# Depthwise convolution taps split into ScalarE products and 1024-column VectorE additions in a two-layer hybrid decoder trunk

## The chip, the cores and the metric

One core of a Trainium2 chip runs the whole program. The metric is the device time of one execution in microseconds (us). Engines are written as in the profile: PE is TensorE (PEld its weight loads), DVE is VectorE, ACT is ScalarE, POOL is GpSimd and SP is SyncE, which issues most loads.

## What is computed

Two layers, each a pre-normalised mixer with three branches that read the same input, then one output projection into the residual; at the end a last RMS norm. Sequence 256, width 2048, everything float32.

```python
h = rms_norm(x, norm_w)
proj = h @ w_in
(qa, ka, va, za, qi, ki, wi, ub, zb, qc, kc, vc, zc, gates) = jnp.split(proj, split_points(), axis=-1)
...
y_a = (dsa_attention(qa, ka, va, qi, ki, wi, top_k) * jax.nn.silu(za)) @ w_a_out
y_b = (conformer_conv(ub, conv_w, conv_b, cln_w, cln_b) * jax.nn.silu(zb)) @ w_b_out
...
y_c = (stick_breaking_attention(qc, kc, vc) * jax.nn.silu(zc)) @ w_c_out
merged = g[:, :, 0] * y_a + g[:, :, 1] * y_b + g[:, :, 2] * y_c
return x + merged @ w_out
```

Branch B is the one that the change touches:

```python
def conformer_conv(u, conv_w, conv_b, ln_w, ln_b):
    a, gt = jnp.split(u, 2, axis=-1)
    y = a * jax.nn.sigmoid(gt)
    y = lax.conv_general_dilated(y, conv_w.astype(y.dtype), window_strides=(1,),
                                 padding=[(CONV_WIDTH - 1, 0)],
                                 dimension_numbers=('NWC', 'WIO', 'NWC'),
                                 feature_group_count=CONV_CH) + conv_b
    y = layer_norm(y, ln_w, ln_b)
    return jax.nn.silu(y)
```

The convolution is depthwise and causal, 31 taps wide, over 1024 channels: for each channel, 31 shifted copies of a row of 256 time steps, each times one weight, are added up, and a bias with them.

## The kernel before

**Weight units.** All projections stream their weights through SBUF in units of 128 partitions x 1024 columns. `load_unit` issues the load on SP into one of five `raw` buffers. `high` (L251, ACT) casts the unit to the matmul's rounded type: `wh`. `low` (L255, DVE) subtracts that from `raw` and so gets the remainder `wl`; `split` uses the same two lines on activations (names `ph`, `pl`, `s`), and L584 and L585 are the two lines for narrower tiles. Three buffers of `wh` and three of `wl` exist. For each unit PE runs 8 matmuls with `wh` and 4 with `wl`, of 512 columns, mostly into `acc` (L265).

**Order of the work.** The program is written out in the order of the units; each counts up `count[0]`. The tile framework orders each engine's instructions from it, and sets the waits between engines. Work that is not projections (norms, rotary embedding, index scores, top-k, softmax, gates) is put between the units: `background` calls generators at a count that each of them names, `tails` and `pending` do the same for work that is due by a certain unit, and `issue_after` ties an instruction behind the newest cast, subtraction or matmul. An engine runs its own instructions in order: whatever stands ahead of a cast or of a subtraction holds it.

**The taps.** The gated input of the convolution lies in `yT` with channels on partitions: 8 channel tiles of 128 channels x (30 zeros + 256 steps). `cv` holds the result, 128 x 8 x 256. `tap` (L645, L647) is one DVE instruction for one channel tile and one tap: it multiplies the shifted row by the weight's column and adds the result in place. `use_u(0)` and `use_u(1)`, one for each half of the channels, put 124 taps each on the list `waiting` in groups of one or two; `drain`, called by `low` after each subtraction, issues one group behind that subtraction. While the index queries are projected (from the line `hold[0] = True` until the projection of the attention queries has been written) `drain` gives out nothing. `flush` empties the list ahead of the layer norm, `conv_norm`.

**The norm of the convolution.** `conv_norm` sums `cv` over its 8 channel tiles with two reductions (L1305) and an addition, lets PE sum over partitions, subtracts the mean, squares on ACT, sums again in two reductions (L1316), and then scales, adds a bias and gates: `AF.Sigmoid` on ACT (L1330), scale and bias on DVE (L1331).

**Later uses named below.** L1034 and L1035 find the largest index scores of each query. L1078 holds the index score matmuls that read the split index query. L1256 is an exponential of the stick-breaking branch, L1385 the sigmoid of a merge gate; L1273 is the matmul that reads that branch's `ph` and `pl`.

Of the kernel before, what the change touches and what calls it, by code (L numbers as in the profile page):

```python
# [10 lines left out]
AF = mybir.ActivationFunctionType  # L11
# [15 lines left out]
PRE = 2  # L27
LATER = 10
# [20 lines left out]
def trunk(ctx: ExitStack, tc: tile.TileContext, x, w_in, xt, w_a, w_b, w_c, w_out,  # L49
# [43 lines left out]
    def slot(dt=F32):  # L93
        return sp.tile([P, KC, S], dt, tag="s8", bufs=13, name=nm("s8"))
# [44 lines left out]
    def t4():  # L139
        return tp.tile([P, 1024], F32, tag="t4", bufs=4, name=nm("t4"))  # L140
# [61 lines left out]
    hold = [False]  # L202

    def drain(after):
        if hold[0]:
            return
        while waiting and waiting[0][0] <= 0:
            with tc.issue_after(after.ins):
                for f in waiting.pop(0)[1]:
                    f()  # L210
            break
        for it in waiting:
            it[0] -= 1

    def flush():
        with tc.issue_after(newest_parts[1].ins):
            while waiting:
                for f in waiting.pop(0)[1]:
                    f()
# [421 lines left out]
    def tap(yT, cv, pr, c, q):  # L641
        wq = pr[:, P_CW + c * TAPS + q:P_CW + c * TAPS + q + 1]
        o = cv[:, c, :]
        if q == 0:
            nc.vector.tensor_scalar(o, yT[:, c, 0:S], wq, pr[:, P_CB + c:P_CB + c + 1], op0=ALU.mult, op1=ALU.add)  # L645
        else:
            nc.vector.scalar_tensor_tensor(o, yT[:, c, q:q + S], wq, o, op0=ALU.mult, op1=ALU.add)  # L647
# [41 lines left out]
    for layer in range(DEPTH):  # L689
# [220 lines left out]
        cv = slot()  # L910

        def taps(j, yT=yT, cv=cv, pr=pr):
            ops = []
            for c in range(j * 4, j * 4 + 4, 2):
                for q in range(TAPS):
                    for d in range(2):
                        ops.append(partial(tap, yT, cv, pr, c + d, q))
            while ops:
                n = 1 + (len(waiting) % 3 > 0)
                waiting.append([4, ops[:n]])  # L920
                ops = ops[n:]
# [27 lines left out]
        hold[0] = True  # L949

# [151 lines left out]
        hold[0] = False  # L1102
# [197 lines left out]
        def conv_norm(cv=cv, pr=pr):  # L1300
            work = t4()
            red = [work[:, i * S:(i + 1) * S] for i in range(4)]
            sums = red[2:]
            for i in range(2):
                nc.vector.tensor_reduce(red[i], cv[:, i * 4:i * 4 + 4, :].rearrange("p c t -> p t c"), op=ALU.add, axis=AX.X)  # L1305
            nc.vector.tensor_add(red[0], red[0], red[1])
            vs = mean_parts(red[0])
            yield 3
            ps = mm_tile()
            summed_parts(ps[:, :S], vs)  # L1310
            for i in range(2):
                cs = cv[:, i * 4:i * 4 + 4, :]
                nc.vector.tensor_sub(cs, cs, heads(ps[:, :S], 4))
                sq = t4()
                nc.scalar.activation(sq.rearrange("p (c t) -> p c t", c=4), cs, AF.Square)
                nc.vector.tensor_reduce(sums[i], sq.rearrange("p (c t) -> p t c", c=4), op=ALU.add, axis=AX.X)  # L1316
            nc.vector.tensor_add(sums[0], sums[0], sums[1])
            vs = mean_parts(sums[0])
# [4 lines left out]
            for i in range(2):  # L1323
# [3 lines left out]
                for c in range(4):  # L1327
                    cc = i * 4 + c
                    lw, lb = pr[:, P_LW + cc:P_LW + cc + 1], pr[:, P_LB + cc:P_LB + cc + 1]
                    nc.scalar.activation(sg[:, c * S:(c + 1) * S], cs[:, c, :], AF.Sigmoid, bias=lb, scale=lw)  # L1330
                    nc.vector.tensor_scalar(cs[:, c, :], cs[:, c, :], lw, lb, op0=ALU.mult, op1=ALU.add)  # L1331
# [306 lines left out]
```

## Time and profile before

| | |
|---|---|
| Median of 3 runs | 2005.81 us (2004.96, 2005.81, 2007.60) |
| Profiled execution, span from first to last instruction | 2003.1 us |
| Profiled execution's own time beside its span | none is listed; the runs lie 1.9 to 4.5 us above this span |
| PE busy | 1993.5 us, 9314 matmuls |
| DVE busy | 1646.5 us, 2179 instructions |
| ACT busy | 1107.4 us, 1275 instructions |
| POOL busy | 200.5 us |
| Mean granted TensorE clock | 0.999 |
| DMA | 463.80 MB, mean 232 GB/s |

The span is what the profile covers; a run's time includes what lies around it. Engines overlap, so busy times do not add up. Busy time of a matmul is modelled and matmuls overlap. In a row of a timeline, a start and a duration stand first; an instruction's record can begin a little before the one ahead of it on the same engine has ended. Idle time in brackets is what the engine waited just before, and for whom.

### The profile page before, as it was taken

To read this page: it belongs to the slowest core of one execution; us is meant where nothing else is said; L and a number is where in the kernel's file an instruction comes from. 1 tells how busy PE (TensorE), PEld (TensorE's weight loads), DVE (VectorE), ACT (ScalarE), POOL (GpSimd) and SP (SyncE) were. 2 spreads that over 40 slices of the span, in tenths; PEclk is the share of its full clock that TensorE was granted. 3 is DMA by queue.
4 is the path that set the end of the run, shared out by engine and by line. 5 is a ranking of instruction groups with operands and counts; after the bars stand their busy time and mean duration, and the time that the engine had idled before them with its cause. 6 is when DMAs were issued, how large, how long until landed. Compare 5 with 4: busy or idle time off the path is not lost.

```text
span 2003.1 us, 25866 instructions
## 1 busy us (share of the span) xinstructions
PE 1993.5 (100%) x9314; PEld 1674.2 (84%) x9314; DVE 1646.5 (82%) x2179; ACT 1107.4 (55%) x1275; POOL 200.5 (10%) x308
## 2 busy tenths in 40 slices
PE   9999999999999999999999999999999999999998
PEld 8889888888888888888888988888888888888886
DVE  8667899878888877798785779988888788778997
ACT  7555555566644455565554555555656445555654
POOL 0111012100010001022110111121000100011120
PEclk9999999999999999999999999999999999999999
DMA  7788578755575567789977885787555765687894
GB/s 279 229 286 266 185 223 291 247 179 186 174 222 192 189 219 253 244 256 281 299 254 231 278 256 184 231 284 247 179 178 173 227 193 190 216 272 241 266 300 160
DMA packets 235585, 463.80 MB, mean 232 GB/s; under 512 B 17280, under 2 KB 30080, under 8 KB 235328
## 3 DMA queue, kind: packets, MB, share of 16 engines
q1 hardware_dynamic: 208768, 389.25, 59.7%
q0 software_dynamic: 25024, 69.75, 12.4%
q10 hardware_dynamic: 1664, 3.15, 0.4%
q8 instruction: 73, 1.20, 0.2%
q14 instruction: 56, 0.46, 0.1%
HBM read 429.31 MB, written 32.77 MB: 231 GB/s over the span
## 4 chain that ended last, share of the span: by engine, by line
PE 98%; DMA 1%; DVE 1%; issue 0%; POOL 0%; ACT 0%; DVEq 0%; POOLq 0%
PE acc L265 80%; PE mm L265 15%; DMA z<-zt 1%; PE mm L1078 1%; PE mm L1168 0%; DMA zy<-z 0%; PE mm L1136 0%; PE mm L1273 0%; PE mm L1219 0%; PE mm L837 0%; DVE wl L255 0%; PE mm L1249 0%; PE mm L1278 0%; PE mm L1222 0%; PE mm L1139 0%
## 5 line engine op out<-in xcount | busy, mean ns | idle before, releaser
L265 PE MATMUL acc<-wh,s 128*128 128x512 f32 (+1 forms) x4712 | 1165.8, 389 | 0.0
L251 ACT CAST wh<-raw 128x1024 fp32r<-128x1024 f32 (+1 forms) x667 | 697.9, 1048 | 704.2 <-PE acc L265 489.8
L255 DVE TENSOR_TENSOR wl<-raw,wh 128x1024 fp32r<-128x1024 f32 (+1 forms) x668 | 808.6, 1213 | 265.0 <-ACT wh L251 262.2
L265 PEld LDWEIGHTS acc<-wh,s 128*128 128x128 f32 x4712 | 876.9, 188 | 172.9 <-issue 0.2
L265 PE MATMUL acc<-wl,s 128*128 128x512 f32 (+1 forms) x2164 | 575.7, 388 | 0.3 <-DVE wl L255 0.3
L265 PEld LDWEIGHTS acc<-wl,s 128*128 128x128 f32 x2164 | 405.7, 188 | 82.6 <-DVE wl L255 0.7
L297 POOL DMA_DIRECT2D z<-zt x180 | 106.1, 602 | 1297.0 <-DVE zt L294 942.2
L647 DVE SCALAR_TENSOR_TENSOR s<-yT,cst,s 128x256 f32<-128x256 f32 x480 | 211.9, 477 | 0.0
L265 PE MATMUL mm<-wh,s 128*128 128x512 f32 x544 | 139.4, 389 | 0.0
L265 PEld LDWEIGHTS mm<-wh,s 128*128 128x128 f32 x544 | 102.1, 188 | 21.2
L265 PE MATMUL mm<-wl,s 128*128 128x512 f32 x272 | 77.7, 389 | 0.0
L265 PEld LDWEIGHTS mm<-s,wl 128*128 128x128 f32 x512 | 66.9, 191 | 5.0
L265 PE MATMUL mm<-s,wl 128*128 128x192 f32 x512 | 66.0, 271 | 0.0
L251 ACT CAST wh<-s 128x1024 fp32r<-128x1024 f32 x43 | 45.3, 1052 | 27.5 <-PE mm L265 13.3
L265 PEld LDWEIGHTS mm<-wl,s 128*128 128x128 f32 x272 | 51.1, 188 | 10.6
L303 POOL DMA_DIRECT2D zy<-z x50 | 36.1, 722 | 236.3 <-DMA z<-zt 72.7
L255 DVE TENSOR_TENSOR wl<-s,wh 128x1024 fp32r<-128x1024 f32 x43 | 52.4, 1218 | 8.9 <-ACT wh L251 8.6
L294 DVE STREAM_TRANSPOSE zt<-acc 128x512 f32<-128x512 f32 (+1 forms) x68 | 45.3, 679 | 9.4 <-PE acc L265 9.4
L251 ACT CAST ph<-raw 128x1024 fp32r<-128x1024 f32 x31 | 32.7, 1054 | 26.8 <-PE mm L265 14.6
L265 PE MATMUL mm<-ph,s 128*128 128x512 f32 x176 | 45.5, 390 | 0.0
L255 DVE TENSOR_TENSOR pl<-raw,ph 128x1024 fp32r<-128x1024 f32 x31 | 37.8, 1218 | 6.9 <-ACT ph L251 6.9
L265 PEld LDWEIGHTS mm<-ph,s 128*128 128x128 f32 x176 | 33.0, 188 | 7.2 <-issue 0.4
(293 smaller groups left out, 1378.9 us busy)
## 6 DMA issues: line engine op xcount, KB each, us to landing
raw<-in_w_in_dram SPq DMA_DIRECT2D x535, 512.0 KB, 4.3
raw<-in_w_out_dram SPq DMA_DIRECT2D x56, 512.0 KB, 6.6
zy<-z POOLq DMA_DIRECT2D x48, 512.0 KB, 5.1
z<-zt POOLq DMA_DIRECT2D x172, 128.0 KB, 4.3
raw<-in_w_a_dram SPq DMA_DIRECT2D x32, 512.0 KB, 3.6
raw<-in_w_c_dram SPq DMA_DIRECT2D x32, 512.0 KB, 4.3
raw<-in_w_b_dram SPq DMA_DIRECT2D x32, 512.0 KB, 5.7
s<-in_w_in_dram SPq DMA_DIRECT2D x16, 512.0 KB, 5.5
```

Of the source, the lines that this page charges most:

```text
L251: newest_parts[0] = nc.scalar.copy(u[1], u[0])
L255: newest_parts[1] = sub = nc.vector.tensor_sub(u[2], u[0], u[1].bitcast(F32))
L265: newest[0] = nc.tensor.matmul(o, lhsT, rhs, start=start, stop=stop, skip_group_check=True)
L294: nc.vector.transpose(tmp[:, t].rearrange("p b k i -> p k b i"), src.rearrange("p k (b c) -> p k b c", b=4, c=32))
L297: nc.gpsimd.dma_start(z[:, :, :, a, :].rearrange("t b c e -> c (t b) e"), tmp[a * 32:(a + 1) * 32].rearrange("c t b k i -> c (t b) (k i)"))
L303: nc.gpsimd.dma_start(y.rearrange("p (t a) k i -> p t (a k i)", a=4), z.rearrange("t b c a e -> (b c) t (a e)"))
L647: nc.vector.scalar_tensor_tensor(o, yT[:, c, q:q + S], wq, o, op0=ALU.mult, op1=ALU.add)
L1078: nc.tensor.matmul(ps[:, q * S:(q + 1) * S], qi[i][:, hd, :], ki[j][:, 0, :], start=n == 0, stop=n == 2)
```

## The change

A tap is no longer one DVE instruction. A step of `waiting` handles one tap of one half: four ACT activations multiply the four channel tiles (128x256 each) by their weight columns into one half of a new tile `products` (one more slot of the pool of 13 that `slot` takes from; the tap's parity chooses the half), and one DVE addition of 1024 columns adds the products of the tap before to `cv`. The first tap's products, with the bias, go straight into `cv`. `drain` issues a step every third unit (`TAP_GAP`), and the hold during the index queries is gone, so that the 64 steps of a layer are spread over it. `conv_norm` sums by folding: an addition of 1024 columns, then of 512 and 256, in place of two reductions and an addition. The last scale and bias move from DVE to ACT. After the change the lines of the helpers stand 4 or 5 earlier: the cast is L246, the subtraction L250, matmuls L260, narrower splits L579 and L580, the products L641 and L643, the tap additions L919, the folds L1300 and L1303.

```diff
--- before.py
+++ after.py
@@ -25,6 +25,7 @@
 TOPK = 64
 TAPS = 31
 PRE = 2
+TAP_GAP = 3
 LATER = 10
 URGENT = 10 ** 6
 PAD = TAPS - 1
@@ -199,24 +200,18 @@
         while stages:
             advance(stages[0])
 
-    hold = [False]
+    due = [0]
 
     def drain(after):
-        if hold[0]:
-            return
-        while waiting and waiting[0][0] <= 0:
+        if waiting and count[0] >= due[0]:
+            due[0] = count[0] + TAP_GAP
             with tc.issue_after(after.ins):
-                for f in waiting.pop(0)[1]:
-                    f()
-            break
-        for it in waiting:
-            it[0] -= 1
+                waiting.pop(0)()
 
     def flush():
         with tc.issue_after(newest_parts[1].ins):
             while waiting:
-                for f in waiting.pop(0)[1]:
-                    f()
+                waiting.pop(0)()
 
     newest = [None]
     newest_parts = [None, None]
@@ -638,13 +633,14 @@
         for k in range(0, KC, 4):
             chunk_F(w, c0 + k * P, hx, KD, partial(use, k), LATER + more if k else LATER - 1)
 
-    def tap(yT, cv, pr, c, q):
-        wq = pr[:, P_CW + c * TAPS + q:P_CW + c * TAPS + q + 1]
-        o = cv[:, c, :]
-        if q == 0:
-            nc.vector.tensor_scalar(o, yT[:, c, 0:S], wq, pr[:, P_CB + c:P_CB + c + 1], op0=ALU.mult, op1=ALU.add)
-        else:
-            nc.vector.scalar_tensor_tensor(o, yT[:, c, q:q + S], wq, o, op0=ALU.mult, op1=ALU.add)
+    def tap_products(dst, yT, pr, j, q):
+        for i in range(4):
+            c = j * 4 + i
+            wq, y = pr[:, P_CW + c * TAPS + q:P_CW + c * TAPS + q + 1], yT[:, c, q:q + S]
+            if q:
+                nc.scalar.activation(dst[:, i, :], y, AF.Copy, scale=wq)
+            else:
+                nc.scalar.activation(dst[:, i, :], y, AF.Identity, scale=wq, bias=pr[:, P_CB + c:P_CB + c + 1])
 
     def x_squares(xc, ssq, q, ts, offset=URGENT):
         n = xc[0].shape[-1]
@@ -908,17 +904,21 @@
         yT = long_tile("yT")
         nc.vector.memset(yT[:, :, 0:PAD], 0.0)
         cv = slot()
-
-        def taps(j, yT=yT, cv=cv, pr=pr):
-            ops = []
-            for c in range(j * 4, j * 4 + 4, 2):
-                for q in range(TAPS):
-                    for d in range(2):
-                        ops.append(partial(tap, yT, cv, pr, c + d, q))
-            while ops:
-                n = 1 + (len(waiting) % 3 > 0)
-                waiting.append([4, ops[:n]])
-                ops = ops[n:]
+        products = Lazy(1, slot)
+
+        def taps(j, yT=yT, cv=cv, pr=pr, products=products):
+            cs = cv[:, j * 4:j * 4 + 4, :]
+
+            def home(q):
+                return products[0][:, q % 2 * 4:q % 2 * 4 + 4, :] if q else cs
+
+            def step(q):
+                if q < TAPS:
+                    tap_products(home(q), yT, pr, j, q)
+                if q > 1:
+                    nc.vector.tensor_add(cs, cs, home(q - 1))
+
+            waiting.extend(partial(step, q) for q in range(TAPS + 1))
 
         def use_u(j, y, yT=yT):
             nc.scalar.copy(blocks(yT[:, j * 4:j * 4 + 4, PAD:]), by_feature(y))
@@ -946,8 +946,6 @@
         qi0 = slot().rearrange("p a b -> p (a b)")
         ks = slot(F32R)
         ki = [ks[:, i:i + 1, :] for i in range(2)]
-        hold[0] = True
-
         indexed = []
 
         def use_i(h, e, y, qi=qi, qi0=qi0, indexed=indexed):
@@ -1099,7 +1097,6 @@
 
         for h in range(0, NH, 4):
             chunk_F(w, O_QA + h * P, hx, KD, partial(use_a, h), LATER if h else LATER - 1)
-        hold[0] = False
         qcT = slot()
 
         def use_q(h, y, qcT=qcT):
@@ -1298,24 +1295,26 @@
                 nc.tensor.matmul(ps, ones_r, v, start=i == 0, stop=i == 1)
 
         def conv_norm(cv=cv, pr=pr):
-            work = t4()
-            red = [work[:, i * S:(i + 1) * S] for i in range(4)]
-            sums = red[2:]
-            for i in range(2):
-                nc.vector.tensor_reduce(red[i], cv[:, i * 4:i * 4 + 4, :].rearrange("p c t -> p t c"), op=ALU.add, axis=AX.X)
-            nc.vector.tensor_add(red[0], red[0], red[1])
-            vs = mean_parts(red[0])
+            def folded(dst, a, b):
+                n = a.shape[-1]
+                nc.vector.tensor_add(dst[:, :n], a, b)
+                while n > S:
+                    n //= 2
+                    nc.vector.tensor_add(dst[:, :n], dst[:, :n], dst[:, n:2 * n])
+                return dst[:, :S]
+
+            flat = cv.rearrange("p c t -> p (c t)")
+            vs = mean_parts(folded(t4(), flat[:, :1024], flat[:, 1024:]))
             yield 3
             ps = mm_tile()
             summed_parts(ps[:, :S], vs)
+            sqs = []
             for i in range(2):
                 cs = cv[:, i * 4:i * 4 + 4, :]
                 nc.vector.tensor_sub(cs, cs, heads(ps[:, :S], 4))
-                sq = t4()
-                nc.scalar.activation(sq.rearrange("p (c t) -> p c t", c=4), cs, AF.Square)
-                nc.vector.tensor_reduce(sums[i], sq.rearrange("p (c t) -> p t c", c=4), op=ALU.add, axis=AX.X)
-            nc.vector.tensor_add(sums[0], sums[0], sums[1])
-            vs = mean_parts(sums[0])
+                sqs.append(t4())
+                nc.scalar.activation(sqs[i].rearrange("p (c t) -> p c t", c=4), cs, AF.Square)
+            vs = mean_parts(folded(sqs[0], *sqs))
             yield 6
             ps = mm_tile()
             summed_parts(ps[:, :S], vs)
@@ -1328,7 +1327,7 @@
                     cc = i * 4 + c
                     lw, lb = pr[:, P_LW + cc:P_LW + cc + 1], pr[:, P_LB + cc:P_LB + cc + 1]
                     nc.scalar.activation(sg[:, c * S:(c + 1) * S], cs[:, c, :], AF.Sigmoid, bias=lb, scale=lw)
-                    nc.vector.tensor_scalar(cs[:, c, :], cs[:, c, :], lw, lb, op0=ALU.mult, op1=ALU.add)
+                    nc.scalar.activation(cs[:, c, :], cs[:, c, :], AF.Identity, bias=lb, scale=lw)
                 nc.vector.tensor_mul(cs, cs, sg.rearrange("p (c t) -> p c t", c=4))
```

How ACT's instructions stand in the index stage, where the hold was. Before (`wh` casts of units, copies of rotary embedding at L961 and L962, index scores at L1051; `s8_134` takes the high part of a turned index query):

```order
L251 CAST wh_338_2009<-raw_337_2007 128x1024
L251 CAST wh_345_2042<-raw_344_2040 128x1024
L961 COPY t4_340_2028<-t4_292_1757 64x768
L962 COPY t4_340_2028<-t4_292_1757 64x768
L251 CAST wh_352_2087<-raw_351_2085 128x1024
L251 CAST wh_360_2128<-raw_359_2126 128x1024
L584 CAST s8_134_850<-t4_292_1757 128x512
L251 CAST wh_363_2146<-raw_362_2144 128x1024
L1051 ACTIVATE t4_350_2075<-mm_349_2066 128x1024
```

The same stretch with the change (L641 is a product into `s8_126`, the new tile; L579 the same high part):

```order
L246 CAST wh_339_2100<-raw_338_2098 128x1024
L246 CAST wh_346_2138<-raw_345_2136 128x1024
L959 COPY t4_341_2124<-t4_293_1833 64x768
L960 COPY t4_341_2124<-t4_293_1833 64x768
L641 ACTIVATE s8_126_793<-yT_75_527,cst_75 128x256
L246 CAST wh_353_2183<-raw_352_2181 128x1024
L641 ACTIVATE s8_126_793<-yT_75_527,cst_75 128x256 x3
L246 CAST wh_361_2224<-raw_360_2222 128x1024
L579 CAST s8_135_856<-t4_293_1833 128x512
L246 CAST wh_364_2247<-raw_363_2245 128x1024
L1049 ACTIVATE t4_351_2171<-mm_350_2162 128x1024
L641 ACTIVATE s8_126_793<-yT_75_527,cst_75 128x256 x2
```

One group of four products (1 + 3) and half of the next one now stand among the casts, where there was none; each cast behind a product runs after it.

DVE at the same place. Before (L585 takes the low part of that index query, from L968's result; L294 turns a projection for a transposition; `sc` are index scores):

```order
L968 TENSOR_TENSOR t4_292_1757<-t4_292_1757,t4_340_2028 128x4x128
L294 STREAM_TRANSPOSE zt_341_2031<-acc_313_1870 128x4x4x32
L255 TENSOR_TENSOR wl_361_2129<-raw_359_2126,wh_360_2128 128x1024
L294 STREAM_TRANSPOSE zt_341_2031<-acc_313_1870 128x4x4x32
L585 TENSOR_TENSOR s8_135_851<-t4_292_1757,s8_134_850 128x512
L255 TENSOR_TENSOR wl_364_2147<-raw_362_2144,wh_363_2146 128x1024
L1055 TENSOR_SCALAR sc_347_2064<-t4_350_2075,wi2_143_863 128x128
```

With the change (L919 is the addition of a tap's products into `cv`):

```order
L966 TENSOR_TENSOR t4_293_1833<-t4_293_1833,t4_341_2124 128x4x128
L289 STREAM_TRANSPOSE zt_342_2127<-acc_314_1951 128x4x4x32
L250 TENSOR_TENSOR wl_362_2225<-raw_360_2222,wh_361_2224 128x1024
L289 STREAM_TRANSPOSE zt_342_2127<-acc_314_1951 128x4x4x32
L250 TENSOR_TENSOR wl_365_2248<-raw_363_2245,wh_364_2247 128x1024
L580 TENSOR_TENSOR s8_136_857<-t4_293_1833,s8_135_856 128x512
L919 TENSOR_TENSOR s8_76_529<-s8_76_529,s8_126_793 128x1024
L1053 TENSOR_SCALAR sc_348_2160<-t4_351_2171,wi2_144_869 128x128
```

The low part stood between two subtractions, ahead of `wl_364`; now it stands behind that subtraction (here `wl_365`), and a tap addition follows it ahead of the scores.

ACT in the tail of the first stick-breaking head group. Before (`ph` is the high part that L1273 waits for, L1385 the sigmoid of a merge gate, with the load of its table):

```order
L251 CAST wh_747_4364<-raw_746_4362 128x1024
L584 CAST ph_741_4349<-t4_675_3956 128x512
L1256 ACTIVATE t4_677_3966<-t4_677_3966 128x768
L251 CAST wh_750_4383<-raw_749_4381 128x1024
L584 CAST ph_741_4349<-t4_677_3966 128x512
L251 CAST wh_753_4403<-raw_752_4401 128x1024
L1385 ACT_TABLE_LOAD
L1385 ACTIVATE ev_743_4357<-acc_710_4162 128x512
L251 CAST wh_757_4441<-raw_756_4439 128x1024
```

With the change:

```order
L246 CAST wh_748_4464<-raw_747_4462 128x1024
L579 CAST ph_742_4449<-t4_676_4059 128x512
L246 CAST wh_751_4487<-raw_750_4485 128x1024
L1253 ACTIVATE t4_678_4069<-t4_678_4069 128x768
L641 ACTIVATE s8_126_793<-yT_75_527,cst_75 128x256 x3
L246 CAST wh_754_4505<-raw_753_4503 128x1024
L1384 ACT_TABLE_LOAD
L1384 ACTIVATE ev_744_4457<-acc_711_4266 128x512
L246 CAST wh_758_4541<-raw_757_4539 128x1024
L1384 ACTIVATE ev_745_4458<-acc_711_4266 128x512
L579 CAST ph_742_4449<-t4_678_4069 128x512
L641 ACTIVATE s8_126_793<-yT_75_527,cst_75 128x256
```

The second `ph` cast stood ahead of the cast of `wh_753`; now it stands behind that cast (`wh_754`), three products, the table load, two sigmoids and the cast of `wh_758`. PE's instructions stand in the same order before and after, and so do SP's.

## Rows read from the trace of the kernel before

**Rows 1.** Page, part 1: busy us (share of the span) and instructions of each engine.

```profile
PE 1993.5 (100%) x9314; PEld 1674.2 (84%) x9314; DVE 1646.5 (82%) x2179; ACT 1107.4 (55%) x1275; POOL 200.5 (10%) x308
```

**Rows 2.** Page, part 4: the chain that ended last, by engine, share of the span.

```profile
PE 98%; DMA 1%; DVE 1%; issue 0%; POOL 0%; ACT 0%; DVEq 0%; POOLq 0%
```

**Rows 3.** Waits of PE: engine line waited for: us, times, longest us.

```profile
PE mm L837 <- DVE eps L73: 1.1, 1, 1.1
PE acc L265 <- DVE wl L255: 0.3, 1, 0.3
```

**Rows 4.** Busy times by stretch: columns as in the first line, x is instructions.

```profile
core 0: us, PE busy (x) PEld busy (x) DVE busy (x) ACT busy (x) POOL busy (x), PEclk, DMA share, GB/s
50.00:240.00 190.00, 190.00 (x1026) 166.44 (x1025) 140.16 (x193) 103.86 (x119) 24.48 (x40) 1.00 0.76 244
260.00:280.00 20.00, 20.00 (x90) 16.56 (x89) 20.00 (x36) 10.01 (x11) 2.32 (x4) 1.00 0.70 212
440.00:450.00 10.00, 10.00 (x46) 8.26 (x45) 7.59 (x11) 9.81 (x12) 0.00 (x0) 1.00 0.44 139
740.00:760.00 20.00, 20.00 (x90) 16.57 (x89) 11.00 (x11) 9.46 (x10) 1.81 (x3) 1.00 0.76 249
```

**Rows 5.** Timeline 262 to 276 us: start, us, instruction, idle before and its releaser.

```profile
263.68 1.06 ACT L251 CAST wh<-raw 128x1024 fp32r<-128x1024 f32 x1 [1.66 <-PE acc L265]
264.38 1.98 PE L265 MATMUL acc<-wh,s 128*128 128x512 f32 x8
266.95 1.22 DVE L255 TENSOR_TENSOR wl<-raw,wh 128x1024 fp32r<-128x1024 f32 x1
269.82 1.98 PE L265 MATMUL acc<-wh,s 128*128 128x512 f32 x8
271.63 1.07 PE L265 MATMUL acc<-wl,s 128*128 128x512 f32 x4
```

**Rows 6.** Groups by line and shape: count, busy us, mean ns, idle before and releasers.

```profile
L255 DVE TENSOR_TENSOR wl<-raw,wh 128x1024 fp32r<-128x1024 f32 x652 | 792.8, 1218 | 256.2 <-ACT wh L251 253.4
L251 ACT CAST wh<-raw 128x1024 fp32r<-128x1024 f32 x651 | 684.1, 1052 | 687.8 <-PE acc L265 475.1 <-DVE s L647 108.2 <-PE mm L265 41.2
L647 DVE SCALAR_TENSOR_TENSOR s<-yT,cst,s 128x256 f32<-128x256 f32 x480 | 211.9, 477 | 0.0
L1305 DVE TENSOR_REDUCE t<-s 128x256 f32<-128x1024 f32 x4 | 8.1, 2018 | 0.1
L777 ACT ACTIVATE s<-s,x0n 128x256 fp32r<-128x256 f32 x15 | 6.8, 497 | 0.8 <-DMA s<-in_xt_dram 0.8
L645 DVE TENSOR_SCALAR s<-yT,cst 128x256 f32<-128x256 f32 x16 | 6.3, 403 | 0.0
L1331 DVE TENSOR_SCALAR s<-s,cst 128x256 f32<-128x256 f32 x16 | 5.8, 407 | 0.0
```

**Rows 7.** Timeline of ACT, 8 to 24 us.

```profile
15.29 0.89 ACT L777 ACTIVATE s<-s,x0n 128x256 fp32r<-128x256 f32 x2
```

**Rows 8.** Timeline 478 to 500 us, the stick-breaking tail.

```profile
484.71 0.61 ACT L584 CAST ph<-t 128x512 fp32r<-128x512 f32 x1
485.98 0.69 DVE L585 TENSOR_TENSOR pl<-t,ph 128x512 fp32r<-128x512 f32 x1
487.27 1.28 ACT L1385 ACT_TABLE_LOAD   x1
488.56 0.60 ACT L1385 ACTIVATE ev<-acc 128x512 f32<-128x512 f32 x1
494.84 0.19 PEld L1273 LDWEIGHTS mm<-ph,vah 128*128 128x128 f32 x1
```

**Rows 9.** Timeline 216 to 224 us, the first index scores.

```profile
218.77 0.65 DVE L585 TENSOR_TENSOR s<-t,s 128x512 fp32r<-128x512 f32 x1
222.96 1.13 PEld L1078 LDWEIGHTS mm<-s,s 128*128 128x128 f32 x8
```

## The prediction

> **What bounds the kernel now.** I read first the busy shares, then the chain of waits, then what PE waits for, and last the engines stretch by stretch.
>
> PE is busy 1993.5 of 2003.1 us; DVE has 82% and ACT 55% of the span [rows 1]. The chain that ended last is 98% PE, with ACT, POOL and DMA together about 1% [rows 2]. In the whole execution PE waits on another engine twice, 1.1 and 0.3 us [rows 3]; the other idle time, 8 us, is the start and the end of the kernel, where nothing of the change stands. So a term counts only if it makes PE wait, or takes one of those 1.4 us away.
>
> The stretches say the same. With DVE busy all of a 20 us stretch PE finishes 90 matmuls, and with DVE at 11.00 us it finishes 90 too [rows 4]. PE is at clock 1.00 (the 2.4 GHz level) in each of them, so there is no clock to win back.
>
> What keeps PE fed is the lead of the two producers. ACT casts a weight unit (wh), DVE subtracts (wl), PE runs 8 + 4 matmuls; three buffers of each. In the DVE-saturated stage the cast that starts at 263.68 had waited 1.66 us for PE: it waits for the buffer that PE has just left [rows 5]. PE then takes the two units already cast (from 264.38, one each 2.72 us), so this one is used at 269.82. The cast ends at 264.74: **a lead of 5.1 us**. DVE's subtraction of the same unit runs only at 266.95 to 268.17, since DVE is full, and PE reads it at 271.63: **a lead of 3.5 us**. That is the thinnest place the taps of before leave. A new delay of ACT under 5 us, or of DVE under 3.5 us, costs nothing; beyond that it costs PE microsecond for microsecond.
>
> **The change, part by part.** One execution is the base: its span is 2003.1 us; the median of the runs shown, 2005.81, lies 2.7 us above, and I carry those 2.7 along.
>
> *Taps off DVE.* 480 fused taps (211.9 us) and 16 first taps (6.3 us) go [rows 6]. In their place come, for each of 2 layers and 2 halves, 30 additions of 1024 columns: 120 x 1.218 us (the wl subtraction has that shape and kind [rows 6]) = 146.2 us. DVE: -72.0 us.
>
> *Norm sums.* Eight reductions go, four of them 8.1 us together and the other four of the same shape [rows 6], 16 us in all; four folds of three additions (1024, 512, 256 columns) come. Each addition is at most 1.218 us, so a fold is 1.2 to 3.7 us and the four 4.9 to 14.6 us; I take 9, as halving columns should roughly halve the variable part. DVE: -7 us.
>
> *Final scale and bias.* 16 operations of 5.8 us move from DVE to ACT [rows 6]. DVE in all: about -85 us, to 1562 us, 78%.
>
> *Products on ACT.* 496 activations of 128x256 with a per-partition scale, and the 16 just named. The nearest row is the same form, an activation with a scale column: 497 ns alone [rows 6], and 0.89 us for two back to back [rows 7], that is 0.40 us more for the second. A group of four costs 0.50 + 3 x 0.40 = 1.7 us; bounds 1.6 and 2.0. 512 x 0.43 = 220 us (205 to 254). ACT: 1107 to 1327 us, 66%.
>
> All these sums are hidden: none lies on the chain, and PE's instructions stand in the same order. **Their term in the time is 0**; the 85 us of DVE buy nothing, and ACT's 220 us cost nothing as long as the leads hold. SP issues the same loads in the same order; POOL's issues trade places once per layer, with no PE work behind them that is near.
>
> The Trainium skill, ScalarE: Activation LUTs, Rules for kernel authors, speaks against this change: multiplication and addition belong on VectorE, not ScalarE. By the rows a tap costs 0.44 us of DVE before (211.9/480), and 0.43 of ACT plus 1.218/4 = 0.30 of DVE after, so engine time does rise by 0.3 us a tap, about 145 us in all, as that rule would have it; what decides the kernel's time is only where it lands.
>
> *Where it lands.* One step comes every 3 units = 8.2 us. ACT gets 1.7 of each 8.2 us, 21% more. Its fullest stretch is 440 to 450, with 9.81 of 10 us [rows 4]; with one group it runs 1.5 us over (2 if a product of another group falls in). A backlog of 2 us against a lead of 5.1: 0. DVE in 260 to 280 loses its taps (some 0.8 us a unit) and gets 0.41 a unit: it becomes 17 us of 20, and the lead of 3.5 us grows. In the index stage, where before no taps ran, DVE has 140.16 of 190 us [rows 4]; it had taps in the first part, and 23 additions add at most 28: 168 of 190. Still under.
>
> *Two places where a step is moved closer to PE's use.* In the index stage the low part of the turned index query now stands behind one more wl on DVE. Before it ends at 219.42 and PE's first matmul with it is after 222.96 [rows 9]: 3.5 us, less 1.2 leaves about 2. In the stick-breaking tail the second ph cast moves behind two casts, the table load, two activations and three products. Before: cast at 484.71, its pl ends at 486.67, PE uses them at 494.84 [rows 8]: 8.2 us. Added: 3 products 1.3, table load 1.28, two activations 1.2, two casts 2.1 and one more wl on DVE 1.2: 7.1 us. Left: 1 us. Each place comes twice, once a layer. Bounds: 0, or, if a buffer wait of one unit (2.72 us) lies between as well, 0.7 us at the one and 1.7 at the other; for the four together 0 to 5 us. I take 0, since the buffer waits that the timeline shows are ACT's idle time and so shrink as it gets more to do.
>
> *The added wait.* Each group of products waits until the addition two steps before it has read its half of the product slot. Behind it on ACT stands the next cast. The addition was issued one unit earlier, so at DVE's normal pace it is done. Cost 0, and if DVE runs late, see the first rival.
>
> Sum: 2003.1 + 0 + 2.7 = 2005.8, **2006 us**.
>
> **Rivals.**
>
> *Slower: ACT stands behind DVE.* ACT runs in order, so a group that waits for a late addition holds the cast, the late cast holds wl, and wl is what the next additions queue behind. It decides where ACT's wait plus 1.7 us exceeds the lead of 5.1 us, so from a wait of 3.4 us, or where wl slips over 3.5 us. For it: DVE is full at 20.00 of 20 in the choose and rotary stage, and its wl there already runs 2 us late. Against it: that stage loses more DVE work than it gets. Price: 60 us a layer, 7 groups, 14 in both layers; 0.5 to 1 us lost for each gives 7 to 14 us: 2013 to 2020 us. At the two moved steps alone, a wait of a whole unit there too (2.7 us beyond what is left, in the two tails, on top of the 5), it is up to 2016. Chance 0.12 together, half of it for the smaller one, 2010 to 2016.
>
> *Faster: the neighbours' traffic slows PE.* If busy DVE and ACT lengthened matmuls, 85 us less of DVE would give time back. A matmul of 512 columns takes 20/90 = 222 ns in these stretches. Rows speak against it: 90 in 20 us at 20.00 and at 11.00 us of DVE [rows 4]. Were one matmul more per 20 us gained in the stretches with taps, 1150 us, it would be 1150/90 = 13 us: 1993. Chance 0.03. The Trainium skill, TensorE: Matmul & The Clock Gate, Wait — 56ns, not 53.3ns?, gives 215.7 ns start to start for 512 columns; if that were reached here by some 8,000 such matmuls, it would be an estimated 50 us, but no row here shows a stretch at that pace.
>
> *The change does not free what it says.* If the extra slot, one more tile in a pool of 13, holds up a writer, DVE and ACT shift but PE's lead pays first; past it, a few us as in the small case above. If the products cost 1 us each rather than 0.43, ACT would reach 1107 + 512 = 1619 us, 81%: still under PE, 2006. Chance of a time outside the band from this: 0.01, counted with slower.
>
> **How the numbers follow.** A measurement of this kernel tells about 0.2%, 4 us, from no change. The forecast, 2006, has 0.83 with a range of 2003.5 to 2008.5, from the runs' own scatter and part of the 0 to 5 us of the four places. Slower by more than 4 us, over 2009.8: 0.12 and the 0.01 of the last rival, 0.13. Faster by more than 4 us: 0.04. The range for 8 in 10 takes in the forecast and the edge of the smaller slower case, where all four places pay: 2003.5 to 2010.5.
>
> **What would show it.** Right: PE at 99 to 100% with the same two short waits; DVE near 1560 us, ACT 1310 to 1360; products near 0.4 to 0.5 us; the four reductions' place taken by additions; the idle time of ACT's cast shorter than 688 us [rows 6] but still released by PE. Wrong: a row in which PE waits for wl or wh, above all at 240 to 300, 440 to 500 and a layer later; a group of matmuls at the index score or the stick tail waiting for DVE; or a 20 us stretch of 512-column matmuls with more or fewer than 90.

## The result, and the profile after

The changed kernel takes 2020.82 us (median of 4 runs, 2020.32 to 2021.52) against 2005.65 us before: ratio 1.0077, 95% interval 1.0063 to 1.0091. It is 15 us slower. The profiled execution has a span of 2018.7 us, 15.6 more than that of before.

The page's busy times and the chain that ended last, after the change (columns as in [rows 1, 2]):

```profile
PE 1999.8 (99%) x9314; PEld 1673.0 (83%) x9314; DVE 1577.5 (78%) x1787; ACT 1301.9 (64%) x1787; POOL 200.5 (10%) x308
PE 90%; DVE 6%; ACT 2%; issue 2%; DMA 1%; DVEq 0%; ACTq 0%
```

DVE lost 69 us of work and ACT got 194; both are further from full than PE. Yet the chain has left PE for 10% of the span. What PE waits for (us, times, longest us; compare [rows 3]):

```profile
PE acc L260 <- DVE wl L250: 4.2, 8, 1.3
PE acc L260 <- ACT wh L246: 3.2, 5, 1.0
PE mm L260 <- DVE s L444: 1.3, 2, 1.0
PE mm L833 <- DVE eps L74: 1.1, 1, 1.1
PE acc L260 <- DVE ev L1358: 0.3, 1, 0.3
PE mm L260 <- DVE wl L250: 0.3, 2, 0.2
```

These are 10.4 us against 1.4 before, so they name the cause's engines but hold only 9.0 of the 15.6 us; another 6.3 us sit in PE's busy time, which rose from 1993.5 to 1999.8 us with the same 9314 matmuls. The full loss is seen by laying the same matmul of both traces side by side. PE's timeline before, single matmul groups outside the weight stream (start, us, instruction):

```profile
30.58 0.50 PE L822 MATMUL mm<-cst,t 128*128 128x1 f32 x4
...
286.14 0.64 PE L1136 MATMUL mm<-s 128*128 128x256 f32 x4
...
1015.49 0.28 PE L720 MATMUL mm<-ph,ones_r 128*128 128x256 f32 x1
...
1281.12 0.76 PE L1136 MATMUL mm<-s 128*128 128x256 f32 x5
...
1703.33 0.28 PE L1298 MATMUL mm<-ph,ones_r 128*128 128x256 f32 x1
```

And the same groups after the change:

```profile
30.46 0.50 PE L818 MATMUL mm<-cst,t 128*128 128x1 f32 x4
...
293.49 0.76 PE L1133 MATMUL mm<-s 128*128 128x256 f32 x5
...
1024.35 0.28 PE L716 MATMUL mm<-ph,ones_r 128*128 128x256 f32 x1
...
1296.16 1.11 PE L1133 MATMUL mm<-s 128*128 128x256 f32 x8
...
1718.38 0.28 PE L1295 MATMUL mm<-ph,ones_r 128*128 128x256 f32 x1
```

The lag is -0.12, 7.35, 8.86, 15.04, 15.05 us. Taken over all matmuls, it grows by 7.5 us between 100 and 282 us and by 6.8 us between 1113 and 1285 us: the index queries and what follows directly, in each layer. From there to the convolution's norm (282 to 700, 1285 to 1700 us) it does not grow by a tenth, though the products go on there at the same pace until 599 us, and until 1602 us in the second layer. The 1.3 us left lie outside the taps.

ACT's waits from 82 to 290 us after the change (engine, line, waited for: us, times, longest), and below them the products' wait over the whole span:

```profile
ACT s L641 <- DVE s L919: 39.8, 19, 6.1
ACT wh L246 <- PE acc L260: 7.4, 7, 1.7
ACT t L959 <- DVE t L957: 5.5, 3, 2.3
...
ACT s L641 <- DVE s L919: 111.8, 60, 6.1
```

Two of ACT's waits over the same stretch before:

```profile
ACT wh L251 <- PE acc L265: 76.8, 61, 3.1
...
ACT t L961 <- DVE t L959: 0.9, 3, 0.4
```

The products wait for the tap additions: 39.8 us in this stretch. The casts, which before waited 76.8 us here, 61 times, for PE to leave a buffer, and so ran ahead of PE as far as they could, now do so for 7.4 us. And the rotary copies (L961 before, L959 after) wait 5.5 us for DVE's rotary result, against 0.9. Here is one place of the loss, in the timeline of ACT and PE after:

```profile
135.83 0.83 ACT L959 COPY t<-t 64x768 f32<-64x768 f32 x1 [2.30 <-DVE t L957]
...
136.67 0.83 ACT L960 COPY t<-t 64x768 f32<-64x768 f32 x1
...
137.53 1.71 ACT L641 ACTIVATE s<-yT,cst 128x256 f32<-128x256 f32 x4
...
139.15 1.03 ACT L246 CAST wh<-raw 128x1024 fp32r<-128x1024 f32 x1
...
140.23 1.65 PE L260 MATMUL acc<-wh,s 128*128 128x512 f32 x6 [0.97 <-ACT wh L246]
```

ACT waits 2.30 us for DVE, copies, runs four products, and only then casts the unit for which PE stands still 0.97 us. This wait is for the rotary result, not for a tap addition; the group behind it did not wait. The same stretch before, with DVE:

```profile
130.83 1.05 ACT L251 CAST wh<-raw 128x1024 fp32r<-128x1024 f32 x1 [0.52 <-PE acc L265]
...
133.99 1.06 ACT L251 CAST wh<-raw 128x1024 fp32r<-128x1024 f32 x1
...
136.80 1.22 DVE L255 TENSOR_TENSOR wl<-raw,wh 128x1024 fp32r<-128x1024 f32 x1
...
137.45 2.00 ACT L251 CAST wh<-raw 128x1024 fp32r<-128x1024 f32 x2
...
138.30 1.56 PE L265 MATMUL acc<-wh,s 128*128 128x512 f32 x6
...
139.69 1.03 PE L265 MATMUL mm<-s,wl 128*128 128x192 f32 x8
...
140.57 1.56 PE L265 MATMUL acc<-wh,s 128*128 128x512 f32 x6
```

A unit here takes PE 2.27 us (138.30 to 140.57), not 2.72. The cast at 130.83 had just got a buffer back and is used three units on, at 136.03; so the one at 133.99 is used at 138.30, and the first of the pair at 137.45, which ends near 138.5, at 140.57. The lead is 3.3 us, then **2.1 us**, with no tap anywhere near. DVE's lead is thinner still: the subtraction at 136.80, for the unit cast at 133.99, ends at 138.02, and PE reads it at 139.69, 1.7 us later.

The largest single wait of PE in the stage shows how a delay builds up over several units. After the change:

```profile
178.04 1.71 ACT L641 ACTIVATE s<-yT,cst 128x256 f32<-128x256 f32 x4 [1.41 <-DVE s L919]
...
180.72 1.23 DVE L250 TENSOR_TENSOR wl<-raw,wh 128x1024 fp32r<-128x1024 f32 x1 [1.58 <-ACT wh L246]
...
183.25 0.83 ACT L959 COPY t<-t 64x768 f32<-64x768 f32 x1 [1.61 <-DVE t L957]
...
184.96 1.83 DVE L963 TENSOR_TENSOR t<-t,cst 128x768 f32<-128x768 f32 x2 [0.61 <-ACT t L960]
...
186.71 1.22 DVE L919 TENSOR_TENSOR s<-s,s 128x1024 f32<-128x1024 f32 x1
...
188.18 1.22 DVE L250 TENSOR_TENSOR wl<-raw,wh 128x1024 fp32r<-128x1024 f32 x1
...
189.45 1.21 PE L260 MATMUL acc<-s,wl 128*128 128x256 f32 x8 [1.28 <-DVE wl L250]
```

A group of products waits 1.41 us for an addition and delays a cast; DVE waits 1.58 us for that cast, so its rotary step comes late and ACT's copies wait 1.61 us for it; the copies are late for DVE in turn, and PE waits for a subtraction behind the rotary step and a tap addition. At this one matmul the lag grows by 1.4 us.

### The profile page after: what moved, and what is told of

Read it like the earlier page. It is cut to its first block, busy times and chain, and to the rows that moved or that the text cites. A ratio compares the mean times of both kernels' runs of the same rounds, so it can differ in the third digit from the quotient of the medians.

```text
span 2018.7 us, 26096 instructions
## 1 busy us (share of the span) xinstructions
PE 1999.8 (99%) x9314; PEld 1673.0 (83%) x9314; DVE 1577.5 (78%) x1787; ACT 1301.9 (64%) x1787; POOL 200.5 (10%) x308
## 4 chain that ended last, share of the span: by engine, by line
PE 90%; DVE 6%; ACT 2%; issue 2%; DMA 1%; DVEq 0%; ACTq 0%
PE acc L260 74%; PE mm L260 13%; DVE wl L250 2%; ACT wh L246 1%; DVE s L919 1%; ACT s L641 1%; DMA raw<-in_w_out_dram 1%; DVE t L963 0%; PE mm L1165 0%; DVE zt L289 0%; DVE sc L1082 0%; DMA raw<-in_w_b_dram 0%; PE mm L1270 0%; PE mm L1216 0%; PE mm L1133 0%
## 5 line engine op out<-in xcount | busy, mean ns | idle before, releaser
L260 PE MATMUL acc<-wh,s 128*128 128x512 f32 (+1 forms) x4712 | 1166.8, 389 | 3.2 <-ACT wh L246 2.6
L250 DVE TENSOR_TENSOR wl<-raw,wh 128x1024 fp32r<-128x1024 f32 (+1 forms) x668 | 808.2, 1213 | 346.5 <-ACT wh L246 344.8
L260 PEld LDWEIGHTS acc<-wh,s 128*128 128x128 f32 x4712 | 876.0, 188 | 178.7 <-ACT wh L246 4.9
L246 ACT CAST wh<-raw 128x1024 fp32r<-128x1024 f32 (+1 forms) x667 | 690.9, 1044 | 423.0 <-PE acc L260 311.4
L260 PE MATMUL acc<-wl,s 128*128 128x512 f32 (+1 forms) x2164 | 576.4, 388 | 1.1 <-DVE wl L250 1.1
L260 PEld LDWEIGHTS acc<-wl,s 128*128 128x128 f32 x2164 | 405.2, 188 | 84.9 <-DVE wl L250 3.3
L641 ACT ACTIVATE s<-yT,cst 128x256 f32<-128x256 f32 x480 | 210.4, 500 | 112.0 <-DVE s L919 111.8
L919 DVE TENSOR_TENSOR s<-s,s 128x1024 f32<-128x1024 f32 x120 | 145.9, 1216 | 0.1
L260 PE MATMUL mm<-wh,s 128*128 128x512 f32 x544 | 139.4, 389 | 0.0
L260 PEld LDWEIGHTS mm<-wh,s 128*128 128x128 f32 x544 | 102.1, 188 | 21.2
L260 PE MATMUL mm<-wl,s 128*128 128x512 f32 x272 | 77.7, 389 | 0.0
L260 PEld LDWEIGHTS mm<-s,wl 128*128 128x128 f32 x512 | 66.6, 191 | 6.3 <-DVE wl L250 1.6
L260 PE MATMUL mm<-s,wl 128*128 128x192 f32 x512 | 66.3, 272 | 0.3 <-DVE wl L250 0.3
L246 ACT CAST wh<-s 128x1024 fp32r<-128x1024 f32 x43 | 45.2, 1052 | 28.6 <-PE mm L260 12.7
L260 PEld LDWEIGHTS mm<-wl,s 128*128 128x128 f32 x272 | 51.1, 188 | 10.6
L250 DVE TENSOR_TENSOR wl<-s,wh 128x1024 fp32r<-128x1024 f32 x43 | 52.4, 1218 | 8.9 <-ACT wh L246 8.6
L246 ACT CAST ph<-raw 128x1024 fp32r<-128x1024 f32 x31 | 32.7, 1054 | 27.0 <-PE mm L260 15.0
L260 PE MATMUL mm<-ph,s 128*128 128x512 f32 x176 | 45.6, 390 | 1.3 <-DVE s L444 1.3
L250 DVE TENSOR_TENSOR pl<-raw,ph 128x1024 fp32r<-128x1024 f32 x31 | 37.8, 1218 | 6.9 <-ACT ph L246 6.9
```

What stands on the lines that cost most here:

```text
L246: newest_parts[0] = nc.scalar.copy(u[1], u[0])
L250: newest_parts[1] = sub = nc.vector.tensor_sub(u[2], u[0], u[1].bitcast(F32))
L260: newest[0] = nc.tensor.matmul(o, lhsT, rhs, start=start, stop=stop, skip_group_check=True)
L641: nc.scalar.activation(dst[:, i, :], y, AF.Copy, scale=wq)
L919: nc.vector.tensor_add(cs, cs, home(q - 1))
```

## The experiments

Four theories were held against each other. A: ACT stands still behind a tap addition, and the casts behind it. B: the products' work, or their length in one piece, is too much for the stage. C: the additions are too much for DVE there. AB, formed after the first eight runs: neither a wait nor a group of products exceeds the lead alone, both ahead of one cast do. Ratios are to the kernel before in the same session.

**The hold put back (e1).** In `drain` the condition `and not hold[0]` again, set over the same lines as before, and a step every second unit.

```diff
-TAP_GAP = 3
+TAP_GAP = 2
...
-        if waiting and count[0] >= due[0]:
+        if waiting and not hold[0] and count[0] >= due[0]:
```

> The changed kernel with the hold during the index queries put back, and a step every second unit instead of every third so that the taps still end before the norm. The PE lag against before grows almost only between 100 and 285 us of each layer, so every theory that puts the loss into the index stage expects about 2006 to 2008 us. If the loss comes from the form of the taps wherever they stand (products and additions as such), it stays near 2020 us, or grows, since the rate elsewhere is 1.5 times as high.

Measured: 2005.62 us, 1.0003 (0.9993 to 1.0013). The whole loss is gone, though steps come 1.5 times as often after the hold. So the form of the taps, the folded sums and the moved scale and bias cost nothing measurable, and the loss belongs to the index stage.

**Two product slots (e2).**

```diff
-        products = Lazy(1, slot)
+        products = Lazy(2, slot)
...
-                return products[0][:, q % 2 * 4:q % 2 * 4 + 4, :] if q else cs
+                return products[q // 2 % 2][:, q % 2 * 4:q % 2 * 4 + 4, :] if q else cs
```

> The changed kernel with two product slots, so that a group of products waits for the addition four steps before and not two. Theory A (ACT stands still behind DVE's addition, and casts stand behind it): the waits of the products for the addition, 112 us, go to near 0, and most of the 15 us comes back: 2006 to 2010 us. Theory B (ACT has too much to do in the index stage) and theory C (DVE has): the waits go, the time stays at 2016 to 2021 us.

Measured: 2020.09 us, 1.0075 (1.0058 to 1.0092); the waits stayed at 111.3 us. The test missed its aim. The order shows why: ACT's groups are moved forward until the buffers are full again, and stand right behind the addition that frees one, as they did with two halves.

**Additions left out (e3).** 

> All additions but the last of each half are left out, so the convolution's sum is missing; ACT's products stay at their places. Theory A: no addition, no wait, 2005 to 2008 us. Theory B (ACT's work): the loss stays, 2016 to 2021 us. Theory C (DVE's work): 2005 to 2008 us, as with A.

Measured: 2073.92 us, 1.0343 (1.0327 to 1.0358), which no theory expected. ACT's timeline shows what happened:

```profile
103.68 3.30 ACT L641 ACTIVATE s<-yT,cst 128x256 f32<-128x256 f32 x8
106.89 1.03 ACT L246 CAST wh<-raw 128x1024 fp32r<-128x1024 f32 x1
107.82 3.30 ACT L641 ACTIVATE s<-yT,cst 128x256 f32<-128x256 f32 x8
```

Eight products between two casts: the line `issue_after` on DVE's subtraction holds only the step's addition. What paces the products in the change is nothing but the wait for their buffer. Without it they crowd into 82 to 180 us, and PE loses 34 us a layer there.

**Products left out (e4).** 

> The products of all taps but the first three are left out, the additions stay, so the convolution's sum is wrong; ACT does not wait for additions any more. Theory A: 2005 to 2008 us. Theory B: 2005 to 2008 us. Theory C (DVE's additions alone hold wl too long in the index stage): 2014 to 2021 us.

Measured: 2005.35 us, 1.0001 (0.9991 to 1.0010). C falls: DVE bears its additions.

**Products tied to a cast (e5).** The only change: a step's products may not go ahead of the cast of its unit.

```diff
-            with tc.issue_after(after.ins):
+            with tc.issue_after(after.ins), tc.issue_after(newest_parts[0].ins):
```

> The changed kernel, in which a group of products is tied behind the cast of the unit of its step; before it was tied to nothing and ran as far ahead as the product slot let it, so that it always stood right behind the addition that frees its half. Nothing is left out. Theory A (ACT waits for the addition with the casts behind it): the waits of products for additions in the index stage fall well below 40 us a layer, and the time to 2005 to 2010 us. Theory B (1.7 us of products in a piece, or ACT's work as such, is too much between the casts of the index stage): the waits fall, the time stays at 2013 to 2021 us.

Measured: 2005.26 us, 1.0002 (0.9992 to 1.0012). The stretch 82 to 290 us by windows (us; then busy us of PE, PEld, DVE, ACT, POOL, each with its instructions; clock, DMA share, GB/s), first the change, then this run, and last this run's wait there:

```profile
82.00:290.00 208.00, 203.70 (x1078) 174.96 (x1077) 178.02 (x241) 143.42 (x218) 26.64 (x44) 1.00 0.75 226
```

```profile
82.00:290.00 208.00, 208.00 (x1117) 181.79 (x1116) 186.70 (x254) 150.86 (x228) 27.36 (x45) 1.00 0.75 237
```

```profile
ACT s L641 <- DVE s L919: 4.5, 2, 3.3
```

ACT and DVE do more here than in the change, and PE is never idle. The sum of the work is not the cause, nor are groups of 1.7 us alone: B falls as it stood. What went is the wait, from 39.8 to 4.5 us, and the groups' places changed with it. At the place of PE's largest wait, DVE still has the addition between the copies and the subtraction:

```profile
177.43 0.83 ACT L959 COPY t<-t 64x768 f32<-64x768 f32 x1
...
180.88 1.22 DVE L919 TENSOR_TENSOR s<-s,s 128x1024 f32<-128x1024 f32 x1
...
182.36 1.22 DVE L250 TENSOR_TENSOR wl<-raw,wh 128x1024 fp32r<-128x1024 f32 x1
```

Copies and subtraction come 5.8 us earlier than in the change, the copies without a wait, and PE does not wait.

**The wait with little work behind it (e6).** Products of 8 columns in place of 256, by the edit from the fourth tap of each half on. 

> The changed kernel with products of 8 columns in place of 256 from the third tap of each half on: the products' waits and their places stay, most of ACT's work goes; the convolution's sum is wrong. Theory A: most of the loss stays, 2012 to 2020 us. Theory B: 2004 to 2008 us.

Measured: 2005.14 us, 1.0000 (0.9990 to 1.0009). The wait is all there:

```profile
ACT s L642 <- DVE s L920: 37.3, 21, 4.4
```

A alone falls too. But a group did not vanish: the 448 small products took 99.4 us, 0.22 us each, so 0.9 us a group against 1.7.

**Four products over three units (e7).** Tied as in e5, handed out 1, 2, 1. 

> As the kernel with products tied to the cast, and a tap's four products handed out over three units (1, 2, 1) in place of four at one unit. Nothing is left out. If the length of a group (1.7 us ahead of a cast) is what exceeds the lead in the index stage: 2004 to 2008 us, below the kernel with groups of four. If ACT's sum of work in the stage decides, or the waits for additions, which are as many: no better than the kernel with groups of four.

Measured: 2006.43 us, 1.0005 (0.9995 to 1.0014), the same as e5. With the wait gone, it makes no difference that these runs could show whether four products stand together or at most two.

**The kernel before without its hold (e8).** `hold[0] = True` taken out. 

> The kernel before with the hold during the index queries taken away, its fused taps on DVE left as they are: it adds 1 or 2 taps of 0.44 us behind each subtraction of that stage, about 0.7 us of DVE a unit of 2.3 to 2.7 us. If that stage bears no background work on DVE either: 2010 to 2025 us. If only ACT's part (products and waits) hurts there: 2004 to 2008 us.

Measured: 2011.42 us, 1.0033 (1.0021 to 1.0045). DVE's fused taps cost there as well, by another way: DVE is busy 199.43 of the 208 us, and PE waits for wl (3.5 us in 6 waits), almost all of it after 250 us, and after 1250 us in the second layer.

**Half-width products (e9).** Also from the fourth tap on. 

> The changed kernel with products of 128 columns in place of 256 from the third tap of each half on (the convolution's sum is wrong): waits as they are, a group of products between the 0.9 us of the 8-column run and the 1.7 us of the change, so about 1.25 us. If wait and group length add up ahead of the cast and PE pays what exceeds the lead (theory AB): part of the 15 us, 2006 to 2015 us. If the group's length has a step at which the stage breaks down, 2005 or 2020 us.

Measured: 2010.83 us, 1.0030 (1.0019 to 1.0040). The wait for additions in the stage is 46.5 us and the group 1.3 us (147.1 us for 448). With waits of 37 to 47 us, groups of 0.9, 1.3 and 1.7 us gave index-stage losses of 0, 4.4 and 14.3 us for both layers: a margin is used up and then exceeded, as AB expects.

**Urgent additions (e10).** `with tc.high_priority():` around the tap addition. 

> The changed kernel with DVE's tap additions made urgent, so that an addition stands on DVE ahead of the other work that is ready; products stay untied, at full length, and nothing is left out. Theory AB: the waits for additions in the index stage (40 us a layer) shorten, and the time falls with them, to 2006 to 2014 us. If not the waits but the place of the groups (right behind the casts, untied) makes the loss: it stays at 2017 to 2021 us. If urgent additions hold wl back instead: PE waits for DVE wl grow, over 2021 us.

Measured: 2022.97 us, 1.0088 (1.0073 to 1.0103). The waits stayed at 40.1 us, probably since the groups stand behind the additions wherever these are, as in e2; and PE waited for a rotated index query (L1047 for DVE, 3.8 us), which the additions had been put ahead of. It decides nothing between the theories.

**Tied and doubled (e11).** Tied as in e5, and each product from the second tap of a half on twice. 

> The kernel with products tied to the cast, each product from the second tap on done twice: ACT's groups are 3.3 us, its work in the index stage grows by another 45 us a layer to about 196 of 208 us. If well placed groups cost nothing up to the full engine: 2004 to 2008 us. Theory AB: 3.3 us ahead of a cast exceeds the stage's lead in places, 2010 to 2040 us, all of the loss in the index stage and next to the stretches with a table load.

Measured: 2014.02 us, 1.0042 (1.0027 to 1.0057). Even with ACT at 187.53 of 208 us in the stage it costs less than the change does with 143.42; 8.8 us of lag grow between 100 and 285 us of the two layers. So work alone does cost, at 3.3 us a group though not at 1.7 (e5).

**Tied, with the wait put back (e12).** All products into one half, behind the addition that has just read it:

```diff
-                return products[0][:, q % 2 * 4:q % 2 * 4 + 4, :] if q else cs
+                return products[0][:, :4, :] if q else cs
...
-                if q < TAPS:
-                    tap_products(home(q), yT, pr, j, q)
                 if q > 1:
                     nc.vector.tensor_add(cs, cs, home(q - 1))
+                if q < TAPS:
+                    tap_products(home(q), yT, pr, j, q)
```

> The kernel with products tied to the cast, but all products of a half go into one buffer, and a step's products come behind its addition, so that every group waits for the addition just before it. Work, number of groups and ties are those of the tied kernel without the wait; nothing is left out. Theory AB (a wait ahead of a full group is what exceeds the lead): waits of products for additions in the index stage come back to 40 us a layer or more, and with them the loss, 2015 to 2030 us. If the tie itself, that is the group's place, was what helped: 2004 to 2009 us in spite of the waits.

Measured: 2018.08 us, 1.0058 (1.0042 to 1.0075). The wait in the stage, and the loss, are back:

```profile
ACT s L641 <- DVE s L917: 45.4, 21, 6.1
```

With e5 and e12 the same products and additions were run without and with the wait: 2005.3 and 2018.1 us. The groups' place moved with the wait, as a group that needs an addition must stand behind it; these two were not separated.

**The leads in these runs.** Each cast and each subtraction can be paired, in order, with the matmuls that use it. The thinnest leads of the units that PE takes up between 82 and 290 us, beside that stretch's waits for additions and the lag that grew in both index stages (all in us):

| run | waits for additions | a group | thinnest lead, cast | thinnest lead, subtraction | lag grown |
|---|---|---|---|---|---|
| before | none | none | 2.1 | 1.7 | |
| e5 | 4.5 | 1.7 | 1.2 | 1.1 | 0 |
| e6 | 37.3 | 0.9 | 1.4 | 0.7 | 0 |
| e9 | 46.5 | 1.3 | 0.3 | 0.05 | 4.4 |
| e11 | 6.0 | 3.3 | 0.05 | 0.05 | 8.8 |
| e12 | 45.4 | 1.7 | 0.05 | 0.05 | 11.9 |
| the change | 39.8 | 1.7 | 0.05 | 0.05 | 14.3 |

A lead of 0.05 us stands where PE had to wait. Where some lead is left, nothing is lost; the loss begins where it is gone. As the traces above show, it is used up over several units and on both producers, so AB's "both ahead of one cast" is too narrow.

## Why the prediction was wrong

**The step that failed** is the one on the lead: "That is the thinnest place the taps of before leave", 3.5 us, "a new delay of ACT under 5 us, or of DVE under 3.5 us, costs nothing". I had measured it where DVE is fullest, at a unit of 2.72 us. In the first part of the index stage a unit is 2.27 us, ACT and DVE hand the rotary copies to each other, and the lead falls to 2.1 us for a cast and 1.7 us for a subtraction with no taps at all. The hold stood over just this stretch. I asked of it only whether the engines' sums fit ("168 of 190. Still under"). They do fit, as e5 shows; the sum is not what decides.

**The second failed step** is the added wait, "Cost 0", since the addition "was issued one unit earlier, so at DVE's normal pace it is done". By the program it even stands a step, three units, earlier. The trace has 111.8 us of such waits, 60 times, up to 6.1 us. I took the order's distance for a distance in time, and did not see that ACT's groups are held by nothing else, so that each of them stands behind its addition at any pace (e2, e3).

**The first rival** had the mechanism, ACT in order behind a late addition with the casts behind it, and a price of 2013 to 2020 us; I gave it 0.12. Its place was wrong: I put it at 240 to 300 us, where 1.8 of layer 0's 7.5 us arose, while 5.6 arose between 100 and 200. With its threshold, a wait of 3.4 us, only three of the 19 waits in layer 0's stage could have paid, 3.4, 5.7 and 6.1 us, all at 240 us or later; at a lead of 2.1 us, by the same working, half a microsecond of wait ahead of a group of 1.7 is enough. That its price ends next to the measured 2020.82 us is luck.

**What held.** The durations. The groups after (count, busy us, mean ns, idle before; compare [rows 6, 7]):

```profile
L641 ACT ACTIVATE s<-yT,cst 128x256 f32<-128x256 f32 x480 | 210.4, 500 | 112.0 <-DVE s L919 111.8
L919 DVE TENSOR_TENSOR s<-s,s 128x1024 f32<-128x1024 f32 x120 | 145.9, 1216 | 0.1
L643 ACT ACTIVATE s<-yT,cst 128x256 f32<-128x256 f32 x16 | 8.5, 593 | 0.1
L1330 ACT ACTIVATE s<-s,cst 128x256 f32<-128x256 f32 x16 | 9.1, 594 | 0.0
```

210.4 + 8.5 + 9.1 = 228 us of activations stand against 220, inside 205 to 254; additions 145.9 against 146.2; ACT 1301.9 against 1327 (and a little under the 1310 to 1360 named as a sign of being right), DVE 1577.5 against 1562, 15 us over; neither difference was followed up. The term 0 for ACT's and DVE's sums was right by e1 and e5, for the norm sums and the moved scale and bias too.

The tail of the stick-breaking branch held as well. The moved cast's low part, and PE's use of it (compare [rows 8]):

```profile
498.83 0.68 DVE L580 TENSOR_TENSOR pl<-t,ph 128x512 fp32r<-128x512 f32 x1
502.19 0.19 PEld L1270 LDWEIGHTS mm<-ph,vah 128*128 128x128 f32 x1
```

2.7 us are left where I had worked out 1, and PE does not wait. The lag does not grow there, nor at the index scores (L1076), where the split had been moved.

The rival of a faster PE fell: from 740 to 760 us PE still does 90 matmuls, and e4 with 1578.6 us of DVE, 68 less than before, is no faster. The Trainium skill's rule (ScalarE: Activation LUTs, Rules for kernel authors) that multiplications belong on VectorE speaks against products on ACT because VectorE is the faster of the two per element (in bf16). The change as it stood did lose 15 us, but not for that reason: at e5's places the products on ACT cost nothing (2005.26 us).

## What to carry to other kernels

Before background work is put into a stage, measure the lead of every producer in that stage, from the end of a cast or subtraction to the matmul that uses it; it differs from stage to stage, and an engine's busy share does not tell it. A wait and the work behind it add up ahead of the next cast on an engine that runs in order, a second producer that exchanges results with it passes the delay on, and PE pays only for what exceeds the lead: here neither the waits with groups of 0.9 us (e6) nor groups of 1.7 us almost without waits (e5) cost anything, and together they cost 15 us. Pace such work by tying each engine's part to that engine's own stream, so that it rarely stands at a buffer that another engine has to free; in e5 this was enough.

## What the runs showed of the hardware that was not expected

A product of 8 columns still takes 290 ns alone and 0.22 us in a row, against 500 ns and about 0.44 us for 256 columns; making it 32 times narrower only halves a group. And PE's waits as listed (10.4 us) hold less than the loss: the rest appears as longer busy time of the same matmuls, so the lag of a matmul between two traces is the surer measure.
